# Two-layer hybrid network on one core: the sum of squares of x taken from GpSimd to ScalarE and VectorE

## The chip, the core and the metric

The kernel runs on one core of a Trainium2 chip, in one launch. The core has a matrix engine (TensorE, PE in the profile, with PEld for its weight loads), VectorE (DVE), ScalarE (ACT), GpSimd (POOL) and SyncE (SP), which here issues most of the transfers. The engines work through their own lists of instructions in order and wait for each other by semaphores. The metric is the time of one execution on the device in microseconds (us); lower is better.

## The reference, cut to what matters

Two layers work on x, which has 512 rows (tokens) of 2048 numbers. Each layer normalises x, projects it, runs two mixers over the projections and adds its output to x. The change is in the normalisation of the first layer, whose factor needs the mean of x squared over the 2048 features:

```python
def rmsnorm(x, g):
    xf = x.astype(jnp.float32)
    y = xf * lax.rsqrt(jnp.mean(xf * xf, axis=-1, keepdims=True) + EPS)
    return (y * g.astype(jnp.float32)).astype(x.dtype)

def even_layer(x, norm_g, w_in, if_bias, qn_g, kn_g, rel_bias, w_out):
    proj = rmsnorm(x, norm_g) @ w_in
    qa, ka, va, za, qb, kb, vb, ob, zb, gif = split_cols(proj, EV_SIZES)
    ...
    return y @ w_out

def reference(x, ...):
    x = x + even_layer(x, ...)
    x = x + odd_layer(x, ...)
    return x
```

## The kernel before, in words

Features lie on the 128 partitions and tokens on the free axis, so x is 16 tiles of 128 x 512. The normalisation is split in two: the gain is multiplied into x before the projection, and the factor 1/sqrt(mean + eps), one number per token, is multiplied into each product when it is taken out of PSUM (the tile `rb`, read in `scaled`). So the projection can begin before the sum of squares is known, and the factor is first needed when the first products are finished.

All matmuls of the projections run in two parts: each operand is split into a rounded high half (`fp32r`, made by ScalarE) and the rest, the low half (made by VectorE as the operand minus its high half). A tile of x is split by `split` (lines 566 and 567 with the gain), a weight tile of 128 x 4 x 128 by `split_weights` (lines 247 and 248). A product takes three matmuls: high by high (line 291), high by low (292), low by high (293). So line 293 of a weight tile waits for line 248 of that tile, and line 292 of a tile of x waits for its line 567.

The first group of the stream is six projections of 128 columns and the gates (a narrow projection of 32 columns, lines 409 to 415). It runs over x in four quarters of four tiles; in each quarter it takes six weight tiles, one for each projection (12 matmuls each), and then the gates. That makes 24 weight tiles, called here the first to the twenty-fourth. The seventh to the twelfth belong to the second quarter. Line 242 multiplies the gain into the weights of the gates.

The sixteen loads of x (line 708) and the first eight splits of weights stand in `layer0` ahead of the stream; the loop there alternates them in a fixed order:

```python
for k in range(KT):
    nc.sync.dma_start(raw[k], a["xT"][:, k, :])
    w_too = k in (0, 3, 4, 5, 6, 7, 9, 11)
    ...
    self.split("x0", k, raw[k], self.col(C_G0 + k))
```

Weight tiles land in 7 buffers (`RAWS`, the tiles `wr`), and a buffer is free for the next load (line 215) when its low half has been made (line 248). SyncE issues all these loads in one order; a load that must wait for a buffer holds up the loads behind it, those of x among them. The last two loads of x stand behind six more loads of weights on that queue.

Everything that is not a projection is a job: a generator that is advanced by one step ("tick") at fixed places of the matmul stream, twice in each weight tile of the first group. What a job writes in one step goes into the engines' lists at that place, between what the stream has written before and after it. `wait("name")` lets as many steps go by as the table `LAG` says. So the order on every engine is fixed by where the steps fall, not by when the data are there. The job `start0` takes the squares and their sum (`acc`); then `row_norm` adds `acc` over the partitions by a matmul with ones (line 636, `row`), and a chain on ScalarE and VectorE makes `rb` of it (`rsqrt`, lines 574 to 584). At `rcol` four tiny matmuls (line 747) turn `rb` into columns.

Of the kernel before, what the change touches and what calls it, by code (L numbers as in the profile page):

```python
# [11 lines left out]
AF = mybir.ActivationFunctionType  # L12
ALU = mybir.AluOpType
# [39 lines left out]
for _h in range(4):  # L53
# [10 lines left out]


LAG = {
    "row0": 20, "row1": 6, "rcol": 8, "gate0": 10, "gate1": 12, "gate.lf": 4, "parts": 1, "silu": 3, "rsqrt": 3,
    "sums": 1, "sums.x0": 40, "sums.y0": 14, "sums.y1": 10, "ml.sm": 2, "vals": 4,
    "conv": 2, "gam": 8, "sv": 8,
    "sv.n": 300,  # L70
# [10 lines left out]
class Net:  # L81
# [651 lines left out]
    def start0(self, raw):  # L733
        nc = self.nc
        yield from self.wait("row0")
        for k in range(KT):
            q = self.tmp() if k else self.acc
            nc.gpsimd.tensor_tensor(q, raw[k], raw[k], ALU.mult)
            if k:
                nc.gpsimd.tensor_tensor(self.acc, self.acc, q, ALU.add)  # L740
            if k % 2:
                yield
        yield from self.row_norm(self.acc)
        yield from self.wait("rcol")
        ps = self.psum("rcol")
        for b in range(4):
            nc.tensor.transpose(ps[:, b : b + 1], self.rb[:1, b * P : b * P + P], self.ident[:1, :1])
        self.rcol = self.cp.tile([P, 8], F32, name="rcol")
        nc.vector.tensor_scalar(self.rcol[:, :4], ps[:, :4], 0.5, None, ALU.mult)
        nc.vector.tensor_scalar(self.rcol[:, 4:], ps[:, :4], 0.25, None, ALU.mult)  # L750
        g = self.gate_rows((yield from self.take("g0")))
        yield from self.mlstm_gates(g)
        yield from self.lam_scale()
        self.tri1 = self.triangle(-NEG, -1)
        yield from self.wait(4)
        self.hgb = self.cp.tile([P, 16], F32, name="hgb")
        nc.vector.tensor_scalar(self.hgb, self.cst[:, C_GBR : C_GBR + 16], 0.5, None, ALU.mult)
        self.onh = self.cp.tile([P, 1], F32, name="onh")
        nc.vector.tensor_scalar(self.onh, self.col(C_ON), 0.5, None, ALU.mult)
# [735 lines left out]
```

## Time and profile before

| | |
|---|---|
| median of 3 runs | 1870.02 us (1868.22 to 1870.05) |
| the profiled execution's own time | 1869.16 us |
| its span | 1867.3 us |
| PE busy | 1833.3 us (98%) |
| DVE busy | 1358.4 us (73%) |
| ACT busy | 868.7 us (47%) |
| POOL busy | 264.7 us (14%) |
| DMA | 232.12 MB, mean 124 GB/s |

The span is the time from the first to the last instruction of the profiled execution; some 1.9 us of its own time lie around it. The page gives the busy share of each engine in 40 slices of 46.7 us: PE shows 7 tenths in the first slice and 9 (90% or more) in all others, and POOL shows 8 in the first slice and 1 in the second. PE is the engine of 78% of the chain that ended last. A busy PE in this profile overlaps: a matmul of 128 x 512 is shown with some 0.39 us, while such matmuls start every 0.23 us when nothing holds them up.

### The profile page before, as it was taken

How to read it: one execution, taken by the hardware profiler on the slowest of the kernel's cores; microseconds unless marked ns; L12 is line 12 of the kernel's file. 1: busy time of each engine (PE TensorE's matmuls, PEld its weight loads, DVE VectorE, ACT ScalarE, POOL GpSimd, SP SyncE). 2: the span in 40 equal slices, each digit the busy share in tenths (PEclk: the TensorE clock that was granted, in tenths of full speed). 3: DMA queues.
4: the chain of work that ended last, by engine and by line, in shares of the span. 5: the costliest groups of instructions: out<-in, count | busy, mean ns of one | idle time of the engine just before them, and what ended most of it. 6: DMA issues, size and time to landing. Idle time of an engine off the chain costs nothing.

```text
span 1867.3 us, 27580 instructions
## 1 busy us (share of the span) xinstructions
PE 1833.3 (98%) x10162; PEld 1567.9 (84%) x10162; DVE 1358.4 (73%) x2352; ACT 868.7 (47%) x1512; POOL 264.7 (14%) x293
## 2 busy tenths in 40 slices
PE   7999999999999999999999999999999999999999
PEld 4789889989889899988899788887788888777998
DVE  8577747797647558788777799889656666768664
ACT  4346435645435355565434544363323334566332
POOL 8101100210110101011011114201212112100000
PEclk9999999999999999999999999999999999999999
DMA  5333423333433333325644435443433333245542
GB/s 184 100 106 109 134 87 119 96 113 116 135 100 106 115 102 108 113 86 187 222 141 149 147 118 169 146 119 103 150 93 114 110 114 110 75 124 166 175 136 74
DMA packets 137287, 232.12 MB, mean 124 GB/s; under 512 B 22896, under 2 KB 32240, under 8 KB 137152
## 3 DMA queue, kind: packets, MB, share of 16 engines
q1 hardware_dynamic: 129488, 208.60, 36.8%
q0 software_dynamic: 5360, 17.57, 2.5%
q10 hardware_dynamic: 2304, 4.20, 0.6%
q8 instruction: 80, 1.31, 0.3%
q14 instruction: 55, 0.45, 0.1%
HBM read 203.79 MB, written 26.51 MB: 123 GB/s over the span
## 4 chain that ended last, share of the span: by engine, by line
PE 78%; DVE 14%; issue 3%; ACT 2%; DMA 2%; SPq 1%; DVEq 0%; ACTq 0%
PE pp L365 38%; PE pp L291 8%; PE pp L293 7%; PE pp L292 7%; DVE act L248 3%; PE pp L427 3%; PE pp L429 3%; PE pp L428 3%; DVE act L1214 1%; ACT act L247 1%; DVE act L567 1%; DVE act L1137 1%; DVE ev L1137 1%; DMA act<-in_xT 1%; SPq L1207 0%
## 5 line engine op out<-in xcount | busy, mean ns | idle before, releaser
L365 PE MATMUL pp<-act,act 128*128 128x256 f32 (+1 forms) x4884 | 794.5, 322 | 0.0
L365 PEld LDWEIGHTS pp<-act,act 128*128 128x128 f32 x4884 | 707.0, 190 | 70.2
L248 DVE TENSOR_TENSOR act<-wr,act 128x512 fp32r<-128x512 f32 x719 | 521.6, 741 | 240.6 <-ACT act L247 237.0
L247 ACT ACTIVATE act<-wr 128x512 fp32r<-128x512 f32 x719 | 418.8, 620 | 200.7 <-DVE wr L222 61.5
L291 PE MATMUL pp<-act,act 128*128 128x512 f32 x960 | 390.3, 407 | 1.3 <-ACT act L563 1.3
L293 PE MATMUL pp<-act,act 128*128 128x512 f32 x960 | 378.1, 394 | 11.8 <-DVE act L248 11.6
L292 PE MATMUL pp<-act,act 128*128 128x512 f32 x960 | 376.9, 393 | 2.7 <-DVE act L567 1.9
L293 PEld LDWEIGHTS pp<-act,act 128*128 128x128 f32 x960 | 181.4, 189 | 54.1 <-DVE act L248 15.1
L291 PEld LDWEIGHTS pp<-act,act 128*128 128x128 f32 x960 | 182.1, 190 | 40.6 <-issue 3.8
L292 PEld LDWEIGHTS pp<-act,act 128*128 128x128 f32 x960 | 181.9, 189 | 38.9 <-DVE act L567 3.2
L427 PE MATMUL pp<-act,act 128*128 128x512 f32 x256 | 100.3, 392 | 0.0
L429 PE MATMUL pp<-act,act 128*128 128x512 f32 x256 | 99.7, 390 | 0.0
L428 PE MATMUL pp<-act,act 128*128 128x512 f32 x256 | 99.7, 389 | 0.0
L222 DVE TENSOR_TENSOR wr<-wr,wr 128x512 f32<-128x512 f32 x111 | 78.0, 703 | 1.3
L980 POOL TENSOR_SCALAR pq<-pq,mx 128x512 f32<-128x512 f32 (+3 forms) x32 | 47.4, 1495 | 188.7 <-DVE mx L977 188.7
L381 ACT ACTIVATE ee<-pp 128x512 f32<-128x512 f32 x74 | 44.0, 594 | 61.5 <-PE pp L365 61.3
L528 POOL DMA_DIRECT2D yd<-ev x20 | 11.4, 568 | 401.6 <-DVE ev L1011 164.5
L784 DVE TENSOR_TENSOR ev<-ev,pp 128x512 f32<-128x512 f32 x32 | 22.0, 687 | 47.6 <-PE pp L365 43.0
L429 PEld LDWEIGHTS pp<-act,act 128*128 128x128 f32 x256 | 48.0, 188 | 10.1
L428 PEld LDWEIGHTS pp<-act,act 128*128 128x128 f32 x256 | 48.1, 188 | 9.7
L427 PEld LDWEIGHTS pp<-act,act 128*128 128x128 f32 x256 | 48.1, 188 | 9.6
L593 ACT ACTIVATE act<-ev 128x512 fp32r<-128x512 f32 x40 | 24.9, 627 | 52.3 <-DVE ev L938 31.0
(334 smaller groups left out, 2033.1 us busy)
## 6 DMA issues: line engine op xcount, KB each, us to landing
wr<-in_wi SPq DMA_DIRECT2D x216, 256.0 KB
wr<-in_ws SPq DMA_DIRECT2D x100, 256.0 KB
wr<-in_wd SPq DMA_DIRECT2D x100, 256.0 KB
wr<-in_wv SPq DMA_DIRECT2D x64, 256.0 KB
wr<-in_wso SPq DMA_DIRECT2D x48, 256.0 KB
wr<-in_wdo SPq DMA_DIRECT2D x48, 256.0 KB
wr<-in_wo SPq DMA_DIRECT2D x32, 256.0 KB
ev<-x1d SPq DMA_DIRECT2D x28, 256.0 KB
```

Source lines behind the costliest of these rows:

```text
L222: sub = lambda o, x, y: nc.vector.tensor_tensor(o, x, y, ALU.subtract)
L247: nc.scalar.activation(h, w, AF.Copy)
L248: nc.vector.tensor_tensor(l, w, h.bitcast(F32), ALU.subtract)
L291: nc.tensor.matmul(ps, h[:, j, :], xh, start=k == 0, stop=False)
L292: nc.tensor.matmul(ps, h[:, j, :], xl, start=False, stop=False)
L293: nc.tensor.matmul(ps, l[:, j, :], xh, start=False, stop=k == KT - 1)
L365: mm = lambda o, x, y, start=False: nc.tensor.matmul(o, x, y, start=start, stop=True, skip_group_check=True)
L381: nc.scalar.activation(e, ps, AF.Copy)
L427: nc.tensor.matmul(ps, xh, h, start=k == 0, stop=False)
L428: nc.tensor.matmul(ps, xh, l, start=False, stop=False)
L429: nc.tensor.matmul(ps, xl, h, start=False, stop=k == KT - 1)
L980: nc.gpsimd.tensor_scalar(rows(b), rows(b), mx[:, 3, b : b + 1], None, ALU.mult)
```

## The change

The squares are taken by ScalarE in place of GpSimd, and added up by VectorE in place of GpSimd. The job begins at the eighth step in place of the twentieth, takes one tile of x per step in place of two, and lets six steps go by (`row1`) before `row_norm`. GpSimd has no instruction left in this job. The numbers computed are the same but for rounding. (Line numbers below are those of the kernel before; in the changed kernel the square stays on line 738 and the addition comes to line 741.)

```diff
 LAG = {
-    "row0": 20, "row1": 6, "rcol": 8, ...
+    "row0": 8, "row1": 6, "rcol": 8, ...
@@ start0
         for k in range(KT):
             q = self.tmp() if k else self.acc
-            nc.gpsimd.tensor_tensor(q, raw[k], raw[k], ALU.mult)
+            nc.scalar.activation(q, raw[k], AF.Square)
+            yield
             if k:
-                nc.gpsimd.tensor_tensor(self.acc, self.acc, q, ALU.add)
-            if k % 2:
-                yield
+                nc.vector.tensor_tensor(self.acc, self.acc, q, ALU.add)
+        yield from self.wait("row1")
         yield from self.row_norm(self.acc)
```

What moves can be read from the order of the instructions on each engine. On ScalarE, behind the splits of the sixteen tiles of x (line 566; `act_221` is the last of them) come the splits of weights (line 247), the eighth tile first (`wr_234`). Before:

```order
L566 ACTIVATE act_221<-act_119,cst 128x512
L247 ACTIVATE act_283<-wr_234 128x512
L247 ACTIVATE act_299<-wr_236 128x512
L247 ACTIVATE act_317<-wr_251 128x512
L247 ACTIVATE act_335<-wr_266 128x512
```

And now:

```order
L566 ACTIVATE act_221<-act_119,cst 128x512
L247 ACTIVATE act_283<-wr_234 128x512
L247 ACTIVATE act_299<-wr_236 128x512
L738 ACTIVATE acc<-act_112 128x512
L738 ACTIVATE tmp_316<-act_112 128x512
L247 ACTIVATE act_320<-wr_251 128x512
L738 ACTIVATE tmp_331<-act_113 128x512
L738 ACTIVATE tmp_340<-act_113 128x512
L247 ACTIVATE act_344<-wr_266 128x512
```

The first square stands behind the split of the ninth weight tile, and from there on the 16 squares lie between the splits of the ninth to the seventeenth.

On VectorE at the same place, the low halves (line 248) of the eighth tile and those behind it. Before:

```order
L567 SCALAR_TENSOR_TENSOR act_221<-act_119,cst,act_221 128x512
L248 TENSOR_TENSOR act_283<-wr_234,act_283 128x512
L248 TENSOR_TENSOR act_299<-wr_236,act_299 128x512
L248 TENSOR_TENSOR act_317<-wr_251,act_317 128x512
L248 TENSOR_TENSOR act_335<-wr_266,act_335 128x512
L248 TENSOR_TENSOR act_346<-wr_281,act_346 128x512
```

And now:

```order
L567 SCALAR_TENSOR_TENSOR act_221<-act_119,cst,act_221 128x512
L248 TENSOR_TENSOR act_283<-wr_234,act_283 128x512
L248 TENSOR_TENSOR act_299<-wr_236,act_299 128x512
L248 TENSOR_TENSOR act_320<-wr_251,act_320 128x512
L741 TENSOR_TENSOR acc<-acc,tmp_316 128x512
L741 TENSOR_TENSOR acc<-acc,tmp_331 128x512
L248 TENSOR_TENSOR act_344<-wr_266,act_344 128x512
L741 TENSOR_TENSOR acc<-acc,tmp_340 128x512
L248 TENSOR_TENSOR act_358<-wr_281,act_358 128x512
```

Ahead of the eighth tile the list is as it was; from the tenth tile on the 15 additions lie between the low halves, the last of them behind that of the sixteenth tile.

On PE only two things move: `row` (line 636) stands 12 matmuls later, in the middle of the fifteenth weight tile in place of the fourteenth, and the four small matmuls of `rcol` (line 747) 12 matmuls later as well. SyncE's list is the same, and so is the order on all engines from there to the end. GpSimd's list loses its 31 instructions of lines 738 and 740.

## Rows read from the trace of the kernel before

**Rows 1.** Busy time by stretch: start and end (us), length, then busy us (instructions) of PE, PEld, DVE, ACT and POOL, the granted clock of PE (1.00 is 2.4 GHz, 0.50 is 1.2 GHz), busy share of the DMA engines, GB/s.

```profile
28.47:43.17 14.70, 5.14 (x25) 2.63 (x23) 14.70 (x11) 5.10 (x9) 14.31 (x11) 0.92 0.18 57
43.17:47.60 4.43, 4.43 (x11) 3.46 (x11) 4.43 (x3) 0.63 (x1) 4.35 (x4) 0.50 0.46 126
47.60:81.00 33.40, 33.40 (x151) 25.19 (x149) 15.28 (x20) 9.53 (x14) 5.94 (x4) 1.00 0.36 117
100.00:1867.00 1767.00, 1747.19 (x9798) 1504.02 (x9796) 1284.64 (x2274) 829.97 (x1453) 216.51 (x254) 1.00 0.40 124
```

**Rows 2.** Waits of PE from 6.4 to 100 us: who waited for whom, us in total, times, longest.

```profile
PE pp L293 <- DVE act L248: 8.3, 3, 4.7
PE pp L292 <- DVE act L567: 1.9, 3, 0.8
PE gates L413 <- DVE ev L242: 1.8, 1, 1.8
```

**Rows 3.** Timeline of PE: start, us, line, operation, and in brackets the idle time before it and what ended it. 6.43 is the first matmul of the first weight tile, 28.47 the first of the gates behind the sixth, 31.64 the first of the seventh, 43.17 the third of the eighth; 47.90 is 11 matmuls behind that one and 53.13 is 22 behind the one at 48.12.

```profile
6.43 0.64 PE L291 MATMUL pp<-act,act 128*128 128x512 f32 x1
...
28.47 0.39 PE L409 MATMUL gates<-act,zeros_r 128*128 128x512 f32 x1
30.65 1.06 PE L413 MATMUL gates<-act,ev 128*32 128x512 f32 x8 [1.79 <-DVE ev L242]
31.64 0.50 PE L291 MATMUL pp<-act,act 128*128 128x512 f32 x1
31.98 0.40 PE L292 MATMUL pp<-act,act 128*128 128x512 f32 x1
...
43.17 0.79 PE L293 MATMUL pp<-act,act 128*128 128x512 f32 x1 [4.69 <-DVE act L248]
...
47.90 0.39 PE L292 MATMUL pp<-act,act 128*128 128x512 f32 x1
48.12 0.39 PE L293 MATMUL pp<-act,act 128*128 128x512 f32 x1
...
53.13 0.39 PE L291 MATMUL pm<-act,act 128*128 128x512 f32 x1
...
63.88 1.02 PE L636 MATMUL row<-acc,ones_r 128*128 128x512 f32 x2
```

**Rows 4.** Timeline of DVE; x3 is three instructions shown as one piece.

```profile
7.17 4.52 DVE L567 SCALAR_TENSOR_TENSOR act<-act,cst,act 128x512 fp32r<-128x512 f32 x3
...
35.33 6.34 DVE L567 SCALAR_TENSOR_TENSOR act<-act,cst,act 128x512 fp32r<-128x512 f32 x4
41.59 14.46 DVE L248 TENSOR_TENSOR act<-wr,act 128x512 fp32r<-128x512 f32 x11
...
69.34 0.69 DVE L581 TENSOR_TENSOR tmp<-tmp,tmp 128x512 f32<-128x512 f32 x1
70.07 0.69 DVE L582 TENSOR_TENSOR tmp<-tmp,tmp 128x512 f32<-128x512 f32 x1
...
71.26 0.69 DVE L584 TENSOR_TENSOR rb<-tmp,tmp 128x512 f32<-128x512 f32 x1
71.87 2.49 DVE L248 TENSOR_TENSOR act<-wr,act 128x512 fp32r<-128x512 f32 x4
81.15 0.69 DVE L453 TENSOR_TENSOR ev<-pp,rb 128x512 f32<-128x512 f32 x1 [6.79 <-PE pp L293]
```

**Rows 5.** Timeline of POOL: the last instruction of this job; the 31 of them follow each other from 4.16 us on.

```profile
52.07 1.63 POOL L740 TENSOR_TENSOR acc<-acc,tmp 128x512 f32<-128x512 f32 x1
```

**Rows 6.** Groups of DVE's instructions by line and shape: count, busy us, mean ns of one, idle before. The first two are of the stretch 8 to 52 us, the third of 56 to 100 us.

```profile
L567 DVE SCALAR_TENSOR_TENSOR act<-act,cst,act 128x512 fp32r<-128x512 f32 x15 | 23.4, 1595 | 0.1
L248 DVE TENSOR_TENSOR act<-wr,act 128x512 fp32r<-128x512 f32 x13 | 21.6, 1697 | 0.0
...
L248 DVE TENSOR_TENSOR act<-wr,act 128x512 fp32r<-128x512 f32 x12 | 7.9, 687 | 2.9 <-ACT act L247 2.8
```

**Rows 7.** SyncE's queue. First the largest of its waits up to 60 us, then its timeline: the time shown is that of the issue, with the waits in it. The loads at 26.41 are those of the last two tiles of x.

```profile
SPq L215 <- DVE act L248: 32.8, 15, 8.0
...
16.95 0.90 SPq L708 DMA_DIRECT2D act<-in_xT  x2
19.72 6.63 SPq L215 DMA_DIRECT2D wr<-in_wi  x3
26.41 0.90 SPq L708 DMA_DIRECT2D act<-in_xT  x2
```

**Rows 8.** Timeline of ACT.

```profile
6.42 2.02 ACT L566 ACTIVATE act<-act,cst 128x512 fp32r<-128x512 f32 x3
...
21.04 1.36 ACT L566 ACTIVATE act<-act,cst 128x512 fp32r<-128x512 f32 x2 [2.05 <-DMA act<-in_xT]
31.55 1.35 ACT L566 ACTIVATE act<-act,cst 128x512 fp32r<-128x512 f32 x2 [9.15 <-DMA act<-in_xT]
32.81 3.22 ACT L247 ACTIVATE act<-wr 128x512 fp32r<-128x512 f32 x6
```

**Rows 9.** DMA traffic from 4 to 22 us in 40 slices of 0.45 us.

```profile
GB/s 273 355 387 373 396 310 232 282 341 319 282 305 364 391 410 414 396 419 391 419 373 401 382 387 396 382 378 392 396 373 387 391 360 337 369 405 360 246 178 278
```

**Rows 10.** Groups of ACT's instructions from 917 to 1060 us, where the second layer takes the same squares on ScalarE.

```profile
L792 ACT ACTIVATE tmp<-ev 128x512 f32<-128x512 f32 x15 | 9.5, 633 | 48.8 <-DVE ev L784 48.8
```

More of the change, by code (lines that the diff above doesn't have):

```diff
@@ L66 @@
 LAG = {
-    "row0": 20, "row1": 6, "rcol": 8, "gate0": 10, "gate1": 12, "gate.lf": 4, "parts": 1, "silu": 3, "rsqrt": 3,
+    "row0": 8, "row1": 6, "rcol": 8, "gate0": 10, "gate1": 12, "gate.lf": 4, "parts": 1, "silu": 3, "rsqrt": 3,
     "sums": 1, "sums.x0": 40, "sums.y0": 14, "sums.y1": 10, "ml.sm": 2, "vals": 4,
```

## The prediction

> **What bounds the kernel now.** I read the stretches first, then PE's waits, then the timelines of the engines that PE waits for. From 47.6 us on PE is never idle to 81 us, and from 100 us to the end it is busy for 1747 of 1767 us [rows 1]. The order of the instructions does not change there, so what the change can win or lose lies ahead of 48 us. There PE stands still: its first matmul begins at 6.43 us and the third of the eighth weight tile only at 43.17 [rows 3]. Each of its waits is for VectorE: low halves of weights 8.3 us, low halves of x 1.9, the gates' weights 1.8 [rows 2]. When it starts again it is at half clock (0.50) for 11 matmuls, after a stretch of 14.7 us in which it was busy for 5.1 [rows 1].
>
> VectorE is late because each of its instructions takes 1.6 to 1.7 us from 8 to 52 us, without idle time, and 0.69 once GpSimd is silent [rows 6]. Back to back the same operation takes 2.49 / 4 = 0.62 us at 71.87, and 6.34 / 4 = 1.58 at 35.33 [rows 4]. GpSimd works without a break until 52.07 + 1.63 = 53.7 us, 1.5 to 1.6 us for an instruction [rows 5]. So as long as GpSimd takes squares, VectorE gets through one instruction for each of GpSimd's.
>
> This also holds back the transfers. SyncE waits 32.8 us for VectorE to free weight buffers, and the last two tiles of x stand behind that: they are issued at 26.41 [rows 7] and reach ScalarE at 31.55, after it has waited 9.15 us [rows 8]. ScalarE and VectorE take their lists in order, so the eighth weight tile, which stands behind these tiles of x, gets its high half at 32.81 [rows 8] and its low half from 41.59 on [rows 4].
>
> [...]
>
> **What goes, and what it is worth.** GpSimd's 31 instructions go. Then VectorE follows ScalarE at 0.62 to 0.69 us per instruction [rows 4, 6]. I follow PE through the start with these durations. Its matmuls start every (53.13 - 48.12) / 22 = 0.228 us [rows 3], so a weight tile takes 12 x 0.228 = 2.73 us.
>
> First tile: ScalarE makes the high halves of the second to fourth tile of x from 6.42 to 8.44 [rows 8]. VectorE, which takes until 7.17 + 4.52 = 11.7 for their low halves now [rows 4], is done at 8.44 + 0.69 = 9.1, and two matmuls later the tile is finished, at 9.6. Five more tiles make 9.6 + 5 x 2.73 = 23.2. Each needs one ScalarE and one VectorE instruction, and about one tile of x is split beside it: 1.3 us against 2.73, so they stay ahead of PE. The gates' first part takes 0.3 + (31.64 - 30.65) = 1.3 us [rows 3], to 24.5. The seventh tile takes 0.34 for its first matmul [rows 3] and 11 x 0.228: to 27.4. The eighth tile's third matmul could then start at 27.9.
>
> Is the eighth tile there? The traffic of 10 to 20 us runs at some 385 GB/s [rows 9], or 0.68 us for a load of 256 KB. The pair of x tiles before the last reached ScalarE at 21.04 [rows 8]; behind it come three loads of weights and then the last pair [rows 7]. With SyncE no longer held, five loads at that rate put the last one at 21.04 + 5 x 0.68 = 24.4. The other bound is the issue: the pair before the last is issued by 16.95 + 0.90 = 17.85 [rows 7], five more issues at 0.68 make 21.2, and the pair's own time from issue to ScalarE was 31.55 - 26.41 = 5.1 [rows 7, 8]: 26.3. I take 25.0, nearer to the rate, since SyncE was held up ahead of 16.95 as well. Then 0.67 for the last tile of x and 0.54 for the weight's high half on ScalarE (2.02 / 3, 3.22 / 6) [rows 8] and 0.69 on VectorE end at 26.9, 1.0 ahead of PE. With 26.3 it is 28.2, and PE waits 0.3.
>
> So the third matmul of the eighth tile moves from 43.17 to 27.9. The matmul that stands 11 behind it starts at 47.90 now and would start 11 x 0.228 = 2.5 later, at 30.4, at the clock of 2.4 GHz: PE then has no long wait behind it, and the clock was 1.00 up to 28 us even with the waits of the kernel before [rows 3]. **The gain is 47.90 - 30.4 = 17.5 us.** About 15.3 of it are waits and 2.2 the half clock.
>
> **What is added.** Sixteen squares on ScalarE at 0.63 us [rows 10] and 15 additions on VectorE. Two dependent additions on VectorE begin 70.07 - 69.34 = 0.73 us apart [rows 4]; I take that for each. Behind the eighth tile's low half VectorE has 8 more low halves and 15 additions: 8 x 0.62 + 15 x 0.73 = 15.9 us, so the sum is ready at about 26.9 + 15.9 = 42.8. In the same time ScalarE has 8 splits and 16 squares: 8 x 0.54 + 16 x 0.63 = 14.4 us. PE takes 2.73 us for a weight tile, and between two splits stand at most four squares (2.5 us), so the weights stay ahead. `row` begins at 63.88 now [rows 3] and would at 63.88 - 17.5 + 2.73 (it stands 12 matmuls later) = 49.1: 6 us after the sum is ready. From there `rb` took 71.26 + 0.69 - 63.88 = 8.1 us [rows 3, 4]: 57.2. It is first needed where the first products come out, at 81.15 now [rows 4] and 63.7 then. All of the addition is hidden beside PE, and each cover has over 5 us; if it were gone, PE would stand at `row` or VectorE at the first product for as long as it is short. `rcol` is four tiny matmuls in another place: nothing. From 47.9 us on everything is the same order, 17.5 us earlier.
>
> The profiled execution took 1869.16 us for its span of 1867.3, 0.05% below the median of 1870.02. **The sum is 1869.16 - 17.5 = 1851.7 us.**
>
> **Rivals.** *The last tiles of x come no earlier.* The loads behind them are many, and two loads alone took 5.1 us. If they came at 31.55 as now, the eighth tile would have its high half at 32.81 [rows 8] and its low half 0.69 later, at 33.5 in place of 27.9: 5.6 us of the gain are lost, 1857.3 us. If that wait also brings the half clock back, 2.2 more: 1859.5. Against it speaks that SyncE's wait was for VectorE [rows 7] and that the DMA engines had almost nothing to do from 28 to 43 us (share 0.18) [rows 1].
>
> *Little is won.* VectorE gets faster, but something that I do not see at this stage ends the start as late, or the rest gives the time back: 1866 to 1872 us. PE busy for 99% of the rest speaks against giving back [rows 1], and the rows show no wait of PE up to 100 us for any engine but VectorE [rows 2].
>
> *Slower.* GpSimd is not what slows VectorE in the start; the 1.58 us would be that of its own operands or of the traffic. Then the eighth tile's low half begins at 41.59 as now and the 24 instructions that end with the last addition take 24 x 1.58 = 37.9 us: the sum is ready at 79.5, while `row` would begin at 63.88 + 2.73 = 66.6. PE waits there for 12.9 us: 1882 us, and 1884 with the half clock behind it. It decides from (66.6 - 41.6) / 24 = 1.04 us per instruction. For it speaks that most of the slow stretch is also that of heavy traffic [rows 9]; against it the 1.58 us at 35.33, when DMA was all but idle, and the return to 0.69 once GpSimd has ended [rows 4 to 6].
>
> **How the numbers follow.** The forecast has a chance of 0.78, the late tiles of x 0.13, little won 0.05, slower 0.04. The forecast's own range is 1849.5 to 1855: PE without any wait from 6.43 on would win 0.4 more (9.2 in place of 9.6), the lowest run of before lies 0.9 below the profiled execution and the highest 0.9 above, and 2 or 3 us may be lost where loads come late by part. The late tiles reach to 1859.5, so the range that holds 8 in 10 is 1849.5 to 1859.5. A difference under 0.2% (3.7 us) cannot be told from no change. Faster by more: 0.78 + 0.13 = 0.91; within: 0.05; slower: 0.04.
>
> **What would show it.** In the profile of the changed kernel VectorE's lines 248 and 567 should take about 0.69 us from the start on, the last tiles of x should be on ScalarE by 25 us, the eighth weight tile's low half should be made by 27 us, PE should wait no more than 1 us in all from 10 us on, its clock should stay at 1.00, and `row` should stand at 49 us without a wait for the sum. The prediction is wrong if VectorE stays at 1.5 us without GpSimd, if PE waits for the sum at `row`, or if the first products come out later than 64 us.

## The result, and the profile after

| | before | after |
|---|---|---|
| median on the same chip | 1869.78 us (4 runs, 1868.22 to 1870.05) | 1853.09 us (4 runs, 1851.03 to 1853.82) |
| profiled execution: time, span | 1869.16, 1867.3 us | 1853.82, 1852.0 us |
| PE busy | 1833.3 us (98%) | 1829.2 us (99%) |
| DVE busy | 1358.4 us | 1340.3 us |
| ACT busy | 868.7 us | 877.9 us |
| POOL busy | 264.7 us | 217.5 us |

The changed kernel is faster: ratio 0.9911, 95% interval 0.9895 to 0.9926, or 16.7 us between the medians. The forecast was 1851.7 us. One of the five runs of e5 below took 3669 us, twice as long as its others, for a reason that nothing on record shows; its median and ratio leave that run out.

The stretch ahead of those in [rows 1], of the kernel before:

```profile
6.43:28.47 22.04, 19.11 (x73) 13.07 (x73) 21.97 (x15) 12.69 (x19) 21.46 (x14) 1.00 0.81 275
```

The same stretches of the changed kernel (the last one ends with its shorter span):

```profile
6.43:28.47 22.04, 21.50 (x93) 15.32 (x92) 15.39 (x23) 14.44 (x23) 0.00 (x0) 1.00 0.87 314
28.47:43.17 14.70, 14.50 (x64) 11.27 (x68) 12.95 (x21) 14.10 (x28) 0.00 (x0) 1.00 0.41 126
43.17:47.60 4.43, 4.43 (x25) 3.14 (x18) 4.29 (x7) 0.00 (x0) 0.00 (x0) 1.00 0.47 121
47.60:81.00 33.40, 33.40 (x154) 25.20 (x153) 19.76 (x38) 14.59 (x21) 0.00 (x0) 1.00 0.29 87
100.00:1851.90 1751.90, 1731.50 (x9728) 1490.89 (x9726) 1269.64 (x2251) 823.76 (x1442) 215.41 (x251) 1.00 0.40 123
```

From 28.47 to 43.17 us PE now does 64 matmuls in place of 25, and the stretch behind it, which was at half clock, does 25 in place of 11. The granted clock is 1.00 in each of these stretches.

PE's waits from 6.4 to 100 us, against 12.0 us in [rows 2], are one row:

```profile
PE pp L291 <- ACT act L247: 0.7, 2, 0.5
```

PE's timeline, with the places of [rows 3]: the first matmul, the gates (28.47 before), the seventh tile (31.64), the eighth tile's first and third matmul (the third at 43.17 before), the one 11 behind it (47.90) and `row` (63.88):

```profile
6.14 0.50 PE L291 MATMUL pp<-act,act 128*128 128x512 f32 x1 [0.24 <-ACT act L247]
...
23.72 0.39 PE L409 MATMUL gates<-act,zeros_r 128*128 128x512 f32 x1
...
25.04 0.50 PE L291 MATMUL pp<-act,act 128*128 128x512 f32 x1
...
28.53 0.50 PE L291 MATMUL pp<-act,act 128*128 128x512 f32 x1 [0.47 <-ACT act L247]
...
29.40 0.50 PE L293 MATMUL pp<-act,act 128*128 128x512 f32 x1
...
32.07 0.39 PE L292 MATMUL pp<-act,act 128*128 128x512 f32 x1
...
50.76 1.02 PE L636 MATMUL row<-acc,ones_r 128*128 128x512 f32 x2
```

VectorE's groups from 8 to 52 us, columns as in [rows 6]. The two lines that took 1.6 and 1.7 us take 0.75 and 0.69, and VectorE now has idle time. Up to 28.47 us the DMA engines were as busy as before (0.87, and 0.81 before), so traffic, the cause in the prediction's rival "slower", is not what had slowed VectorE:

```profile
L248 DVE TENSOR_TENSOR act<-wr,act 128x512 fp32r<-128x512 f32 x18 | 12.1, 687 | 1.1 <-ACT act L247 1.0
L741 DVE TENSOR_TENSOR acc<-acc,tmp 128x512 f32<-128x512 f32 x15 | 10.3, 690 | 1.2 <-ACT tmp L738 0.5
L567 DVE SCALAR_TENSOR_TENSOR act<-act,cst,act 128x512 fp32r<-128x512 f32 x14 | 10.1, 752 | 6.1 <-ACT act L566 6.0
```

VectorE's timeline ([rows 4] before): the last low halves of x, the eighth tile's low half with the ninth's, the last two additions, `rb` and the first product (81.15 before):

```profile
27.33 1.42 DVE L567 SCALAR_TENSOR_TENSOR act<-act,cst,act 128x512 fp32r<-128x512 f32 x2 [3.45 <-ACT act L566]
28.66 1.29 DVE L248 TENSOR_TENSOR act<-wr,act 128x512 fp32r<-128x512 f32 x2
...
44.42 1.48 DVE L741 TENSOR_TENSOR acc<-acc,tmp 128x512 f32<-128x512 f32 x2
...
59.45 0.69 DVE L584 TENSOR_TENSOR rb<-tmp,tmp 128x512 f32<-128x512 f32 x1
...
65.30 0.69 DVE L453 TENSOR_TENSOR ev<-pp,rb 128x512 f32<-128x512 f32 x1 [3.35 <-PE pp L293]
```

ScalarE's timeline ([rows 8] before) has the last two pairs of x and the split of the eighth tile, and SyncE's ([rows 7] before) the issue of those pairs:

```profile
21.68 1.41 ACT L566 ACTIVATE act<-act,cst 128x512 fp32r<-128x512 f32 x2 [2.07 <-DMA act<-in_xT]
26.57 1.39 ACT L566 ACTIVATE act<-act,cst 128x512 fp32r<-128x512 f32 x2 [3.48 <-DMA act<-in_xT]
27.86 1.14 ACT L247 ACTIVATE act<-wr 128x512 fp32r<-128x512 f32 x2
```

```profile
16.26 1.02 SPq L708 DMA_DIRECT2D act<-in_xT  x2
17.66 1.69 SPq L215 DMA_DIRECT2D wr<-in_wi  x3
19.64 1.01 SPq L708 DMA_DIRECT2D act<-in_xT  x2
```

The last pair is issued at 19.64 in place of 26.41 and worked on from 26.57 in place of 31.55.

Where the time went: the first product comes 81.15 - 65.30 = 15.85 us earlier, and the span is 15.3 shorter. In all kernels below, the span minus the start of the first product lies between 1784.5 and 1786.9 us. So the whole change is made ahead of the first product, and the rest of an execution scatters over 2.4 us, whichever kernel it is.

### The profile page after: what moved, and what is told of

It reads as the page before. It is cut to its first block, busy times and chain, and to the rows that moved or that the text cites. A ratio compares the mean times of both kernels' runs of the same rounds, so it can differ in the third digit from the quotient of the medians.

```text
span 1852.0 us, 27588 instructions
## 1 busy us (share of the span) xinstructions
PE 1829.2 (99%) x10162; PEld 1566.2 (85%) x10162; DVE 1340.3 (72%) x2367; ACT 877.9 (47%) x1528; POOL 217.5 (12%) x262
## 4 chain that ended last, share of the span: by engine, by line
PE 80%; DVE 12%; issue 3%; ACT 2%; DMA 2%; SPq 1%; DVEq 0%; ACTq 0%
PE pp L365 39%; PE pp L291 8%; PE pp L293 8%; PE pp L292 8%; PE pp L427 3%; PE pp L429 3%; PE pp L428 3%; DVE act L248 3%; DVE act L1214 1%; DMA act<-in_xT 1%; ACT act L247 1%; DVE act L1137 1%; DVE ev L1137 1%; DMA wr<-in_wi 0%; SPq L1207 0%
## 5 line engine op out<-in xcount | busy, mean ns | idle before, releaser
L248 DVE TENSOR_TENSOR act<-wr,act 128x512 fp32r<-128x512 f32 x719 | 507.7, 721 | 242.1 <-ACT act L247 239.6
L784 DVE TENSOR_TENSOR ev<-ev,pp 128x512 f32<-128x512 f32 x32 | 22.0, 688 | 46.9 <-PE pp L365 43.2
```

Of the source, the lines that this page charges most:

```text
L248: nc.vector.tensor_tensor(l, w, h.bitcast(F32), ALU.subtract)
```

## The experiments

The theory to be tested: GpSimd's instructions that read SBUF hold up VectorE's two-input instructions, one for one, and this alone made the start late. The rivals, besides the traffic: GpSimd's activity as such or its writes do it; the late transfers of x were the bound; or the gain comes with the number of instructions taken from GpSimd, wherever they stood.

| kernel | first matmul | `row` | first product | span | median | ratio to before (95%) |
|---|---|---|---|---|---|---|
| before | 6.43 | 63.88 | 81.15 | 1867.3 | 1869.78 | |
| after | 6.14 | 50.76 | 65.30 | 1852.0 | 1853.09 | 0.9911 (0.9895 to 0.9926) |
| e1 | 6.07 | 66.28 | 80.83 | 1867.6 | 1869.37 | 0.9998 (0.9988 to 1.0007) |
| e2 | 6.22 | 50.55 | 65.10 | 1851.4 | 1853.08 | 0.9912 (0.9897 to 0.9926) |
| e9 | 6.14 | 52.74 | 67.37 | 1853.7 | 1856.81 | 0.9936 (0.9921 to 0.9952) |
| e3 | 6.07 | 53.32 | 68.00 | 1853.2 | 1856.81 | 0.9936 (0.992 to 0.9953) |
| e4 | 6.34 | 52.39 | 66.94 | 1853.2 | 1855.82 | 0.9927 (0.9913 to 0.9942) |
| e5 | 6.07 | 50.34 | 64.88 | 1849.4 | 1853.42 | 0.9917 (0.9903 to 0.993) |
| e6 | 5.96 | 64.61 | 81.88 | 1868.7 | 1869.68 | 1.0005 (0.9996 to 1.0013) |
| e7 | 6.14 | 55.27 | 69.81 | 1854.6 | 1856.41 | 0.9932 (0.9919 to 0.9946) |
| e8 | 5.96 | 50.39 | 64.93 | 1851.1 | 1853.22 | 0.9919 (0.9906 to 0.9933) |
| e10 | 6.60 | 49.91 | 64.45 | 1851.3 | 1853.49 | 0.9919 (0.9906 to 0.9933) |
| e11 | 6.10 | 49.89 | 64.44 | 1849.4 | 1852.78 | 0.9915 (0.9901 to 0.9928) |
| e12 | 6.26 | 64.41 | 81.67 | 1868.0 | 1868.3 | 0.9997 (0.9988 to 1.0006) |

Times are in us; the first four columns of numbers are of the profiled execution. Beside e1 to e4 the kernel before had a median of 1869.64 us, beside e5 to e8 1868.75, beside e9 to e12 1868.5. In before, e6 and e12 `row` stands 12 matmuls (2.7 us) earlier in the order.

### Is it GpSimd, and which of its instructions?

**e1: the changed kernel, with 31 two-input instructions of GpSimd like the old ones beside it, into a tile that is overwritten later.**

```diff
         yield from self.wait("row0")
+        for k in range(KT):
+            nc.gpsimd.tensor_tensor(self.rb, raw[k], raw[k], ALU.mult)
+            if k:
+                nc.gpsimd.tensor_tensor(self.rb, self.rb, raw[k], ALU.add)
```

> The changed kernel, and GpSimd does 31 products and sums of the tiles of x beside it into a tile that nobody reads yet, as many and of the same shape as before the change. Theory (GpSimd's instructions with two SBUF inputs hold VectorE at one instruction for each of theirs): lines 248 and 567 on VectorE take 1.6 us again until GpSimd ends at about 54 us, the eighth weight tile's low half is made at about 42 us, PE stands still and falls to half clock as before, and the time is back at 1868 to 1872 us. Rival (the gain comes from the shorter way of the squares or from the earlier steps, not from GpSimd's silence): 1853 us, VectorE at 0.7 us.

Measured: 1869.37 us, all of the gain gone. VectorE's groups from 8 to 52 us are those of the kernel before again:

```profile
L567 DVE SCALAR_TENSOR_TENSOR act<-act,cst,act 128x512 fp32r<-128x512 f32 x15 | 22.9, 1554 | 1.4 <-ACT act L566 1.3
L248 DVE TENSOR_TENSOR act<-wr,act 128x512 fp32r<-128x512 f32 x10 | 17.1, 1722 | 0.0
```

So the gain is not in the new place of the squares but in GpSimd's silence. PE's waits here add up to 8.6 us, less than the 12.0 of [rows 2], and yet the time is the same. The stretches (columns as in [rows 1]) say why:

```profile
6.20:28.50 22.30, 20.39 (x74) 14.03 (x73) 20.93 (x15) 12.70 (x19) 20.33 (x14) 0.92 0.82 281
28.50:43.20 14.70, 7.76 (x25) 4.36 (x23) 14.70 (x10) 7.59 (x14) 13.91 (x11) 0.77 0.17 58
43.20:47.60 4.40, 4.26 (x13) 3.36 (x14) 4.40 (x4) 0.00 (x0) 4.21 (x3) 0.67 0.39 122
```

The clock is at 0.92, 0.77 and 0.67, lower than in the kernel before (1.00, 0.92 and 0.50) in the first two. By these shares some 13 us were at half clock here and some 7 in the kernel before (an estimate). What the waits do not take here, matmuls at half clock do.

**e2: GpSimd busy for as long, but only writing.**

```diff
+        for k in range(96):
+            nc.gpsimd.memset(self.rb, 0.0)
```

> The changed kernel, and GpSimd writes zeros into a tile 96 times (128x512, about 0.53 us each, some 50 us from the start on); it reads nothing. Theory as in the first run, narrow form (only a GpSimd instruction that reads SBUF holds VectorE): VectorE at 0.7 us, 1853 us. Wide form (any GpSimd instruction on SBUF does): VectorE at about 1.15 us (0.62 and 0.53 in turn), the eighth tile's low half at about 33 us in place of 29, 1856 to 1860 us.

Measured: 1853.08 us, the same as the changed kernel. GpSimd's timeline, then VectorE's group of the low halves from 8 to 52 us:

```profile
1.76 55.97 POOL L737 MEMSET rb<- 128x512 f32 x96
```

```profile
L248 DVE TENSOR_TENSOR act<-wr,act 128x512 fp32r<-128x512 f32 x18 | 12.1, 687 | 0.8 <-ACT act L247 0.6
```

A GpSimd that only writes, without a break to 57.7 us, leaves VectorE at 687 ns. The rival of activity or writes is out.

**e9: GpSimd reading one operand.**

```diff
+        for k in range(48):
+            nc.gpsimd.tensor_copy(self.rb, raw[k % KT])
```

> The changed kernel, and GpSimd copies tiles of x (128x512, one operand read, one written) 48 times from the start on. If any GpSimd instruction that reads SBUF holds VectorE, VectorE's lines 248 and 567 become longer by about the length of a copy, 1.2 to 1.6 us in all, and the time is 1857 to 1869 us. If only GpSimd's instructions with two operands do, VectorE stays at 0.7 us and the time is 1853 us.

Measured: 1856.81 us, 3.7 more than the changed kernel and just below what was expected; the low halves take 1.04 us, less than the expected 1.2. GpSimd's timeline (the first copy, ahead of VectorE's first instruction), then VectorE's group of the low halves from 8 to 52 us, a piece of its timeline, and the stretch from 28 to 52 us:

```profile
4.10 0.61 POOL L737 COPY rb<-act 128x512 f32<-128x512 f32 x1 [2.28 <-DMA act<-in_xT]
```

```profile
L248 DVE TENSOR_TENSOR act<-wr,act 128x512 fp32r<-128x512 f32 x15 | 15.4, 1039 | 0.0
```

```profile
46.42 1.09 DVE L248 TENSOR_TENSOR act<-wr,act 128x512 fp32r<-128x512 f32 x1
47.44 2.11 DVE L743 TENSOR_TENSOR acc<-acc,tmp 128x512 f32<-128x512 f32 x2
49.47 1.09 DVE L248 TENSOR_TENSOR act<-wr,act 128x512 fp32r<-128x512 f32 x1
```

```profile
28.00:52.00 24.00, 22.77 (x104) 17.57 (x102) 22.74 (x24) 13.59 (x25) 22.58 (x24) 1.00 0.31 90
```

VectorE starts an instruction every (49.47 - 46.42) / 3 = 1.02 us, and from 28 to 52 us each of the two engines has 24 instructions: they take turns. A copy alone takes 0.61 us and VectorE's own pace is 0.62 [rows 4]; turns without any overlap would give 1.23. With e1's squares, the first of which takes 1.04 us alone, the sum is 1.66, and from a square's start to that of the next addition are 1.45 us (25.69 to 27.14); the pace of 1.58 in [rows 4] is the mean of squares and additions. With copies the start stays nearly as fast; what is late is the sum, for which PE waits 2.0 us at `row`. This is the wait of the rival "slower", in small: 24 instructions from 27.90 us (the eighth tile's low half) to a `row` that was due at 52.74 - 1.97 = 50.77 leave (50.77 - 27.90) / 24 = 0.95 us for each, and 1.02 is just past that.

### Half of the change at a time

**e3: squares on ScalarE, additions on GpSimd. e4: squares on GpSimd, additions on VectorE.**

```diff
 e3
-                nc.vector.tensor_tensor(self.acc, self.acc, q, ALU.add)
+                nc.gpsimd.tensor_tensor(self.acc, self.acc, q, ALU.add)
 e4
-            nc.scalar.activation(q, raw[k], AF.Square)
+            nc.gpsimd.tensor_tensor(q, raw[k], raw[k], ALU.mult)
```

> Half of the change: squares on ScalarE, the 15 sums on GpSimd. They cannot begin before the first square at about 29 us. Theory: VectorE is at 0.7 us until then, so the eighth tile comes at 28.7 as in the changed kernel; behind it low halves take 1.5 us, which PE's 2.73 us for a tile hides, and GpSimd's chain of 15 x 1.6 us ends at about 53 us, 2 us behind the place of the sum's matmul (50.8): 1853 to 1857 us. Rival (the number of GpSimd's instructions sets the loss, wherever they lie): about half of the gain, 1861 us.

> The other half: squares on GpSimd, sums on VectorE. The first seven squares run from 4 to about 15 us and then GpSimd must wait for free tiles until VectorE adds, from about 31 us on. Theory: VectorE is at 1.6 us from 4 to 15 us only, PE loses about 2 us at the first tiles, VectorE has caught up when it waits for the late tiles of x, and the other nine squares go beside PE: 1854 to 1858 us. Rival (the number of GpSimd's instructions sets the loss, wherever they lie): about half of the gain, 1861 us.

Measured: 1856.81 and 1855.82 us. If the gain came with the number of instructions, each half would keep about half of 16.7 us; each keeps over 12. The largest of PE's waits in e3 and in e4, from 6.1 to 100 us:

```profile
PE row L636 <- POOL acc L741: 2.9, 1, 2.9
```

```profile
PE pp L292 <- DVE act L567: 1.4, 3, 0.5
```

In e3 GpSimd's first addition starts at 29.5 us, when the eighth tile's low half is made; VectorE's low halves slow to 1.03 us on the mean, but none is waited for, and it is GpSimd that is late with the sum. In e4 the slower VectorE makes PE wait three times for low halves of x, 1.4 us in all, and is in time for `row`. Its trace also has both paces next to each other: GpSimd's first seven squares end at 15.40 us, while the DMA engines go on moving 385 GB/s from 15.9 to 23 us (busy share 0.88 on the mean from 6.2 to 28.5). VectorE's low halves on either side:

```profile
14.42 1.53 DVE L248 TENSOR_TENSOR act<-wr,act 128x512 fp32r<-128x512 f32 x1
...
16.53 0.68 DVE L248 TENSOR_TENSOR act<-wr,act 128x512 fp32r<-128x512 f32 x1
```

So what counts is whether GpSimd reads while PE depends on VectorE, and for how long.

Not every instruction of GpSimd that reads SBUF holds VectorE like this. Later in the changed kernel GpSimd multiplies four pieces of a tile by factors, one for each partition (line 980, one tile read). These are GpSimd's timeline and VectorE's low halves from 200.6 to 206.9 us:

```profile
200.61 6.32 POOL L980 TENSOR_SCALAR pq<-pq,mx 128x512 f32<-128x512 f32 x4 [13.71 <-DVE mx L977]
```

```profile
L248 DVE TENSOR_TENSOR act<-wr,act 128x512 fp32r<-128x512 f32 x4 | 2.7, 698 | 1.1 <-ACT act L247 1.1
```

VectorE has eight instructions in this stretch, GpSimd four, and the low halves take 698 ns. One for one is shown for GpSimd's `tensor_tensor` (e1) and `tensor_copy` (e9); why this form differs is open.

### What the added work costs

**e5: the changed kernel without the sum.** 15 of the 16 squares and all 15 additions are left out, so its factor is not that of the reference.

```diff
+            if not k:
+                nc.scalar.activation(self.acc, raw[k], AF.Square)
             yield
-            if k:
-                nc.vector.tensor_tensor(self.acc, self.acc, q, ALU.add)
```

> The changed kernel without 15 of the 16 squares and without the 15 additions: the factor is made of the squares of the first tile alone. Theory (the added work lies wholly beside PE): as the changed kernel, 1852 to 1854 us. Rival (the added instructions delay the weights): up to some us faster than 1851.

Measured: ratio 0.9917 against 0.9911. In its trace the first product stands at 64.88, 0.4 us ahead of the changed kernel. The added work is hidden.

**e8: the sum of squares of the second layer moved from GpSimd to VectorE too.**

```diff
-            nc.gpsimd.tensor_tensor(self.acc, self.acc, q, ALU.add)
+            nc.vector.tensor_tensor(self.acc, self.acc, q, ALU.add)
```

> The changed kernel, and the same move once more: the sum of squares for the second layer (15 additions that lie between 900 and 1060 us) on VectorE in place of GpSimd. Theory: PE is never idle there, so nothing is won though VectorE's instructions get shorter there too: 1852 to 1854 us. Rival (GpSimd beside VectorE costs time everywhere): several us faster.

Measured: 1853.22 us, nothing won. GpSimd's reads there cost no time that can be measured (1853.09 us in the changed kernel).

### Were the late tiles of x the bound?

**e6: the kernel before, with the last two tiles of x loaded early through ScalarE's queue. e7: the same in the changed kernel.**

```diff
-                nc.sync.dma_start(raw[k], a["xT"][:, k, :])
+                if k < 14:
+                    nc.sync.dma_start(raw[k], a["xT"][:, k, :])
+                if k in (5, 7):
+                    nc.scalar.dma_start(raw[14 + k // 7], a["xT"][:, 14 + k // 7, :])
```

> The kernel before, with the last two loads of x issued by ScalarE's queue at about 11 and 13 us, ahead of the weights that held them up. Theory (VectorE's pace is the bound, the late loads only follow from it): ScalarE is done early, but VectorE has no idle time and reaches the eighth weight tile at 41 to 42 us as before: 1868 to 1871 us. Rival (the late tiles of x are the bound): the eighth tile at 33 us or earlier, 1857 to 1861 us.

> The changed kernel with the same two loads early. Theory: the last tiles of x are on ScalarE by about 23 us in place of 26.6, the eighth tile's low half is made by 26 us and PE has no wait there; 0.5 to 1.5 us faster than the changed kernel, 1851.5 to 1852.5 us. Rival (the early loads push back the first weights by as much): 1853 us or more.

Measured: e6 1869.68 us, no gain. Its timelines of ScalarE and VectorE:

```profile
25.57 2.58 ACT L566 ACTIVATE act<-act,cst 128x512 fp32r<-128x512 f32 x4 [2.48 <-DMA act<-in_xT]
```

```profile
35.38 6.33 DVE L567 SCALAR_TENSOR_TENSOR act<-act,cst,act 128x512 fp32r<-128x512 f32 x4
41.62 14.45 DVE L248 TENSOR_TENSOR act<-wr,act 128x512 fp32r<-128x512 f32 x11
```

The last tiles are on ScalarE by 28 us in place of 33, and the low halves of the weights begin at 41.62 as before (41.59 in [rows 4]). VectorE's own list was the bound; the late transfers followed from it.

e7 took 1856.41 us, 3.3 more than the changed kernel: a miss. SyncE's waits, then its timeline (the gates' load, line 202, was issued at 11.52 in the changed kernel):

```profile
SPq L202 <- DMA act<-in_xT: 3.8, 1, 3.8
```

```profile
11.94 1.02 SPq L709 DMA_DIRECT2D act<-in_xT  x2
16.77 0.33 SPq L202 DMA_DIRECT2D ev<-in_wg  x1
```

The gates' load waited for the load of x that ScalarE had issued at 11.26 us, and held up SyncE's queue behind it. The program has eight semaphores for its loads, used in turn, and lets a load go when the earlier one on its semaphore has landed: in the changed kernel's trace the gates' load goes at 11.52 us, and the load of x that was issued at 4.95 on the same semaphore has landed at 11.50. In e7 the earlier load on the gates' semaphore is ScalarE's first. So this wait is one that the program asks for. The last x came to ScalarE at 28.84, later than the 26.57 without the edit, PE waited 2.3 us for the eighth tile's high half, and the clock fell to 0.88 between 28.5 and 43.2 us.

**e10: the changed kernel with the last loads of x ahead of the seventh weight on SyncE's own queue. e11: the changed kernel with the eighth weight tile split ahead of the last tiles of x. e12: as e11, in the kernel before.**

```diff
 e10
-                nc.sync.dma_start(raw[k], a["xT"][:, k, :])
+                for j in range(k, KT if k == 10 else k + 1):
+                    if k <= 10:
+                        nc.sync.dma_start(raw[j], a["xT"][:, j, :])
 e11, e12
-                w_too = k in (0, 3, 4, 5, 6, 7, 9, 11)
+                w_too = k in (0, 3, 4, 5, 6, 7, 9, 11, 12)
```

> The changed kernel with the last five loads of x issued on SyncE's queue ahead of the seventh weight tile and the six loads of weights behind it, none of which PE wants before 25 us. Theory (the 1.5 us that the forecast missed are the late last tiles of x): these are on ScalarE by about 24 us, the eighth tile's low half is made by 27 us, PE does not wait there: 0.7 to 1.5 us faster than the changed kernel, 1851.6 to 1852.5 us. Rival (something else holds the eighth tile): 1853 us.

> The changed kernel with the eighth weight tile loaded and split behind the thirteenth tile of x in place of the sixteenth, on all queues. Theory as in the run before: its low half is made at about 24 us, the ninth tile's at about 29 with PE there at 30; no wait: 1851.6 to 1852.5 us. Rival: 1853 us.

> The same in the kernel before, with GpSimd at its squares. Theory (PE waits for VectorE's list, 1.58 us an instruction): the eighth tile's low half comes at about 38.5 in place of 43.2 us and the ninth's at 43.3; PE then waits for the ninth: 2.5 to 5 us won, 1864 to 1867.5 us. Rival (PE is held by something that the order does not change): 1869 us.

Measured: 1853.49 and 1852.78 us for e10 and e11. In both traces PE has no wait at the eighth tile and `row` stands 0.9 us earlier than in the changed kernel, but e10's first matmul is 0.5 us later, and in the whole time neither can be told from the changed kernel: a microsecond at the start is less than the scatter behind it.

e12 took 1868.3 us: no gain, where 1864 to 1867.5 was expected. Its timelines of VectorE and PE (the ninth tile's third matmul), and two stretches:

```profile
37.67 1.78 DVE L248 TENSOR_TENSOR act<-wr,act 128x512 fp32r<-128x512 f32 x1
```

```profile
45.77 0.79 PE L293 MATMUL pp<-act,act 128*128 128x512 f32 x1 [3.25 <-DVE act L248]
```

```profile
43.20:47.60 4.40, 1.83 (x4) 1.49 (x5) 4.40 (x4) 0.26 (x1) 4.24 (x4) 0.69 0.13 37
45.77:64.41 18.64, 18.64 (x73) 14.22 (x73) 11.19 (x10) 3.18 (x4) 8.59 (x6) 0.84 0.41 141
```

The eighth tile's low half is made at 37.67 + 1.78 = 39.5 us in place of 43.2, and PE then waits for the ninth's. The ninth's third matmul stands at 45.77, 2.35 us ahead of the 48.12 of [rows 3], but now half clock lies behind it (0.84 on the mean up to `row`): from there to `row` it takes 18.6 us, and 63.88 - 48.12 = 15.8 at a clock of 1.00 in the kernel before. These 2.9 us eat the 2.35.

## Why the prediction was right, and where its size was off

- **VectorE's pace without GpSimd: right.** 0.69 us for line 248 and 0.75 for line 567. The rows of before ([rows 4], [rows 6]) show this pace only after GpSimd's last instruction of the job; that it holds from the first tile on, beside the traffic, was the author's estimate, and the changed kernel shows it, with a DMA share of 0.87 up to 28.47 us. e1 brings 1.72 and 1.55 back. e2 and e9 narrow it to instructions that read: line 248 takes 0.69 us beside memsets and 1.04 beside copies. Turns without overlap do not describe it fully: e9's pace is 1.02 us where they would give 1.23, and beside line 980, which reads too, low halves take 698 ns.
- **The late transfers as part of the bound: only half right.** The prediction said that the slow VectorE also holds back the last tiles of x, and that the eighth tile stands behind these. Both are in the rows, but e6 brought the tiles early and won nothing: in the kernel before VectorE's list alone was the bound.
- **The first six tiles and the gates: right within 0.5 us.** 23.72 for 23.2; of this the first tile had 0.36 (the second begins at 9.96 in place of 9.6).
- **The last tiles of x: mis-sized.** The prediction took 25.0 us, with 26.3 as its far bound; ScalarE began with the pair at 26.57. The rate behind the 25.0 is borne out elsewhere: in e9 the pair was issued at 19.64 too, into the same traffic (387 GB/s from 16.26 to 21.68 us in both), and ScalarE began with it (25.03 - 21.67) / 5 = 0.67 us per load after the pair before:

```profile
25.03 1.37 ACT L566 ACTIVATE act<-act,cst 128x512 fp32r<-128x512 f32 x2 [1.95 <-DMA act<-in_xT]
```

  From issue to ScalarE the pair took 5.4 us there, 5.5 in e3, 6.0 in e5, 6.4 in e8, 6.9 in the changed kernel and 7.1 in e2, all with the same order of loads up to it. In the changed kernel the end of this wait was not traffic:

```profile
24.80:26.57 1.77, 1.77 (x11) 1.27 (x8) 0.00 (x0) 0.00 (x0) 0.00 (x0) 1.00 0.18 60
```

  What delayed the last packets is open, so about 1.5 us of this term is scatter that the prediction had no price for. The rest is its count: five loads lead to the first tile of the last pair, and the last tile comes one load later (on ScalarE the two take 27.86 - 26.57 = 1.29 us, where the prediction had 0.67). Its far bound counts the pair's own issue twice: 5.1 us is measured from the start of that issue, 21.2 is its end.
- **The eighth tile: 29.40 in place of 27.9.** 0.5 of it comes from the tiles ahead, the rest from x: 0.47 is shown as PE's wait for the high half. e10 and e11 take this wait away in their traces. So the prediction's 1.0 us to spare there was missing.
- **The clock: right.** 1.00 in all stretches. No run shows the clock in GHz, as [rows 1] and the forecast have it; what the traces show is its share, and a matmul every 0.228 us at 1.00 and every (47.90 - 43.17) / 11 = 0.43 us at 0.50. The matmul 11 behind the third of the eighth tile stands at 32.07 (30.4 forecast, 47.90 before): a gain of 15.83 us in place of 17.5, and that is the 15.85 at the first product. The forecast's 1.7 us too much are the 1.5 at the eighth tile and 0.2 in the pace of the 11 matmuls behind it (32.07 - 29.40 = 2.67 in place of 2.5).
- **The added work: right, hidden.** The sum is ready at 44.42 + 1.48 = 45.9 us, 4.9 ahead of `row` at 50.76 (42.8 and 49.1 forecast); `rb` at 60.1, 5.2 ahead of the first product. e5 shows that leaving it all out wins nothing that can be measured.
- **What was to show it.** PE's 0.7 us of waits are within the 1 us; low halves by 27 us and x by 25 are missed. The first product at 65.30 is past the 64 us at which the prediction called itself wrong: it is 1.6 us behind the forecast 63.7, 1.0 by the late x and 0.5 by the tiles ahead. The rival of the late tiles came true by about 1 us of its 5.6.
- **Back from the start to the whole time.** The prediction let the rest of the order go through unchanged. It does: 1786.2 us before and 1786.7 after, between the first product and the end. So the median's 1.4 us above the forecast go with the 1.7 us missing at the start, though the scatter of the rest (2.4 us) is as large.
- **Slips that change no verdict.** Of the gain it calls 15.3 us waits, while those of [rows 2] add up to 12.0. In the rival of the late tiles 32.81 is the start of the weight's split and not its end, so 33.5 should be 34.0. The clock up to 28 us is not in [rows 3]; the stretch from 6.43 to 28.47 us shown with the result has it.

No version run here is clearly faster than the changed kernel. Left open is which operand of VectorE's instruction is held, since no run took one of its two SBUF operands away, which forms of GpSimd's instructions hold it, and what delays the last packets of x in some traces.

## What to carry to other kernels

When VectorE's two-input instructions slow down to one for each of GpSimd's beside them (here from 0.69 to some 1.7 us), look at what GpSimd reads there before looking at transfers or order. Move that work only where PE depends on VectorE, since elsewhere it may win nothing (e8: 1853.22 against 1853.09 us). A load that arrives late is not shown to be the bound until an early one moves the work behind it; in e6 it did not (low halves from 41.62 us on, and from 41.59 before). Do not build on the time of a load from a single trace: the same pair took 5.4 to 7.1 us from its issue in six traces, and a step that stood 1.0 us ahead of PE in the sum was late for it.

## What had not been expected of the hardware

- GpSimd's memsets, 55.97 / 96 = 0.58 us each, cost VectorE nothing (687 ns for line 248), while copies of nearly the same length (0.61 us) take its pace from 0.62 to 1.02 us. Line 980, which reads one tile as a copy does and runs for 6.32 us in four instructions, leaves the low halves at 698 ns.
- In these runs the half clock moves with the wait: it stands behind the eighth tile's in the kernel before (0.50 from 43.17 to 47.60 us), behind the ninth's in e12 (0.84 on the mean from 45.77 to 64.41), and in several short stretches in e1 (0.92, 0.77, 0.67). In e12 shortening one wait of two won nothing (1868.3 against 1868.5 us), since the other then had half clock behind it.
- Two loads on a second queue made the same transfers later (e7): through a semaphore that the program shared between the queues, a load on SyncE's queue waited 3.8 us for one of ScalarE's.
